# RMSNorm with relu on one core: hardware loops with own semaphores, 32-row chunks in three slots

## The chip, the cores and the metric

One core of one Trainium2 chip. The metric is the device time of one execution in microseconds (us), median of several runs. "Span" is the time from the first to the last instruction in the profile of one execution; it is about 2 us shorter than the device time.

## The reference

```python
def setup_inputs():
    batch, seq, dim = 16, 1024, 512        # x: 16384 rows of 512 float32
    ...
def reference(x, gamma, eps):
    rms = np.sqrt(np.mean(x ** 2, axis=-1, keepdims=True) + eps)
    x_norm = x / rms * gamma
    return np.maximum(x_norm, 0).astype(np.float32)
```

33.55 MB are read and 33.55 MB are written, and little is computed on them.

## The kernel before

128 rows per partition are cut into 8 chunks of 16 rows (one contiguous 32 KB piece per partition), which pass through six slots. A chunk is two groups of 8 rows. SyncE issues all loads and stores of x; ScalarE makes the sums of squares and the square root; VectorE does the rest.

```python
    K = 16; G = 8
    nchunks = rows // K          # 8
    nslots = 6
    junk = psum.tile([P, d], F32, name="junk")       # ONE scratch tile for all squares
    ...
    def compute(i):
        xt = slot[i % nslots]
        for g in range(ngroups):
            a, b = g * G, (g + 1) * G
            for j in range(a, b):
                nc.scalar.activation(out=junk, in_=xt[:, j, :], func=ACTF.Square,
                                     accum_out=ss[i][:, j:j + 1])
            nc.scalar.activation(out=rms[i][:, a:b], in_=ss[i][:, a:b],
                                 func=ACTF.Sqrt, bias=eps_sb, scale=inv_d)
            nc.vector.tensor_mul(out=xt[:, a:b, :], in0=xt[:, a:b, :], in1=gammaG())
            nc.vector.reciprocal(out=rstd[i][:, a:b], in_=rms[i][:, a:b])
            for j in range(a, b):
                nc.vector.tensor_scalar(out=xt[:, j, :], in0=xt[:, j, :],
                    scalar1=rstd[i][:, j:j + 1], scalar2=0.0, op0=ALU.mult, op1=ALU.max)
    # ... gamma: four DMA issues of one row each, then loads and computation of chunks 0 to 5, nxt = 6, then:
    for i in range(nchunks):
        store(i)
        if i >= 1 and nxt < nchunks:
            load(nxt); compute(nxt); nxt += 1
```

Semaphores are placed by the framework, and all of it is straight code.

Of the kernel before, what the change touches and what calls it, by code (L numbers as in the profile page):

```python
# [1 line left out]

# [4 lines left out]

F32 = mybir.dt.float32
ALU = mybir.AluOpType
ACTF = mybir.ActivationFunctionType  # L10


@with_exitstack
def kernel(
    ctx: ExitStack,
    tc: tile.TileContext,
    x: bass.AP,
    gamma: bass.AP,
    eps: bass.AP,
    out: bass.AP,  # L20
):


    nc = tc.nc
    P = nc.NUM_PARTITIONS

    x2 = x.flatten_outer_dims()
    out2 = out.flatten_outer_dims()
    n, d = x2.shape
    rows = n // P  # L30
    inv_d = 1.0 / d
    xv = x2.rearrange("(c p k) d -> c p k d", p=P, k=16)
    ov = out2.rearrange("(c p k) d -> c p k d", p=P, k=16)

    K = 16
    G = 8
    nchunks = rows // K
    nslots = 6
    ngroups = K // G

    singles = ctx.enter_context(tc.tile_pool(name="singles", bufs=1))
    slots = ctx.enter_context(tc.tile_pool(name="slots", bufs=1))
    small = ctx.enter_context(tc.tile_pool(name="small", bufs=1))
    psum = ctx.enter_context(
        tc.tile_pool(name="psum", bufs=1, space=bass.MemoryType.PSUM))

    ctx.enter_context(tc.manual_schedule())

    gseed = singles.tile([P, d], F32, name="gseed")
    gamma_sb = singles.tile([P, d], F32, name="gamma_sb")  # L50
    eps_sb = singles.tile([P, 1], F32, name="eps_sb")
    junk = psum.tile([P, d], F32, name="junk")
    slot = [slots.tile([P, K, d], F32, name=f"slot{s}") for s in range(nslots)]
    ss = [small.tile([P, K], F32, name=f"ss{i}") for i in range(nchunks)]
    rms = [small.tile([P, K], F32, name=f"rms{i}") for i in range(nchunks)]
    rstd = [small.tile([P, K], F32, name=f"rstd{i}") for i in range(nchunks)]

    def load(i):
        nc.sync.dma_start(out=slot[i % nslots], in_=xv[i])

    def store(i):
        nc.sync.dma_start(out=ov[i], in_=slot[i % nslots])

    def gammaG():
        g = gamma_sb[:]
        return bass.AP(tensor=g.tensor, offset=g.offset,
                       ap=[g.ap[0], [0, G], g.ap[1]])

    def compute(i):
        xt = slot[i % nslots]  # L70
        for g in range(ngroups):
            a, b = g * G, (g + 1) * G
            for j in range(a, b):
                nc.scalar.activation(out=junk, in_=xt[:, j, :], func=ACTF.Square,  # L74
                                     accum_out=ss[i][:, j:j + 1])
            nc.scalar.activation(out=rms[i][:, a:b], in_=ss[i][:, a:b],  # L76
                                 func=ACTF.Sqrt, bias=eps_sb, scale=inv_d)
            nc.vector.tensor_mul(out=xt[:, a:b, :], in0=xt[:, a:b, :], in1=gammaG())  # L78
            nc.vector.reciprocal(out=rstd[i][:, a:b], in_=rms[i][:, a:b])  # L79
            for j in range(a, b):  # L80
                nc.vector.tensor_scalar(  # L81
                    out=xt[:, j, :], in0=xt[:, j, :],
                    scalar1=rstd[i][:, j:j + 1], scalar2=0.0,
                    op0=ALU.mult, op1=ALU.max)

    nc.vector.memset(gseed, 0.0)  # L86
    nc.vector.memset(eps_sb, eps)  # L87
    for q in range(0, P, 32):
        nc.scalar.dma_start(out=gseed[q:q + 1, :], in_=gamma[None, :])

    for i in range(min(nslots, nchunks)):
        load(i)
    nc.vector.stream_shuffle(gamma_sb, gseed, [0] * 32)  # L93
    for i in range(min(nslots, nchunks)):
        compute(i)
    nxt = nslots
    for i in range(nchunks):
        store(i)
        if i >= 1 and nxt < nchunks:
            load(nxt)  # L100
            compute(nxt)
            nxt += 1


# [1 line left out]
_INS = ['x', 'gamma', 'eps']  # L106
_OUTS = [((16, 1024, 512), 'float32')]

_NUMBERS = {'eps': 9.999999747378752e-06}


# [26 lines left out]
```

## Time and profile before

| | before |
|---|---|
| device time, median of 3 runs | 164.23 us |
| span | 162.0 us |
| VectorE busy | 124.6 us (77%) |
| ScalarE busy | 98.5 us (61%) |
| DMA engines in packets of x | 96.9% of the span |

The busy share of an engine is an average; what bounds the kernel is read from where a gap would be seen first. The prediction shows those lines (columns of windows: window, length, busy time of VectorE, ScalarE and GpSimd with instruction counts, clock, DMA share, GB/s).

### The profile page before, as it was taken

The page shows a single profiled execution, that of the slowest core. Times are in us where ns is not written, and L with a number is a line of the kernel's source. Part 1 is how long each engine was busy: PE and PEld are TensorE (multiplying, and loading weights), DVE is VectorE, ACT ScalarE, POOL GpSimd, SP SyncE. Part 2 cuts the span into 40 slices and gives each one's busy share as a digit, 9 for nine tenths or more (in the row PEclk, how much of TensorE's full clock was granted, in tenths as well). Part 3 has the DMA queues.
Part 4 walks back from the last instruction along what each step waited for, and adds up shares of the span by engine and source line. Part 5 has one row for each costly group of instructions (what it writes and reads, how often), then busy time and mean ns, then how long its engine had stood idle before and what let it go on. Part 6 is the DMA issues. An engine that isn't in the chain of part 4 may idle for free.

```text
span 162.0 us, 554 instructions
## 1 busy us (share of the span) xinstructions
DVE 124.6 (77%) x164; ACT 98.5 (61%) x274; POOL 0.2 (0%) x4
## 2 busy tenths in 40 slices
DVE  1001299999999999999999999999999999920000
ACT  2107999999999999999999199901998000000000
POOL 0000000000000000000000000000000000000000
DMA  6999899999999999998999999999999999999990
GB/s 227 421 405 502 388 413 493 390 421 477 396 421 471 396 388 388 461 445 388 463 437 404 453 445 404 453 437 396 461 429 445 429 421 445 429 421 445 437 413 16
DMA packets 2315, 67.14 MB, mean 414 GB/s; under 512 B 260, under 2 KB 260, under 8 KB 264
## 3 DMA queue, kind: packets, MB, share of 16 engines
q1 hardware_dynamic: 2304, 67.11, 96.9%
q14 instruction: 3, 0.02, 0.0%
q10 hardware_dynamic: 8, 0.01, 0.0%
HBM read 33.56 MB, written 33.55 MB: 414 GB/s over the span
## 4 chain that ended last, share of the span: by engine, by line
DVE 74%; DMA 8%; ACT 3%; issue 2%; DVEq 0%
DVE slot L78 43%; DVE slot L81 30%; DMA slot<-in_x_dram 8%; ACT junk L74 3%; DVE rstd L79 1%; DVEq L133 0%
## 5 line engine op out<-in xcount | busy, mean ns | idle before, releaser
L74 ACT ACTIVATE junk<-slot 128x512 f32<-128x512 f32 x128 | 76.8, 600 | 23.0 <-DMA slot<-in_x_dram 19.5
L78 DVE TENSOR_TENSOR slot<-slot,gamma_sb 128x4096 f32<-128x4096 f32 x16 | 70.7, 4418 | 4.2 <-ACT junk L74 4.2
L81 DVE TENSOR_SCALAR slot<-slot,rstd 128x512 f32<-128x512 f32 x128 | 52.1, 481 | 0.6
L74 ACT ACTIVATION_READ_ACCUMULATOR junk<-slot 128x1 f32 x128 | 23.8, 186 | 0.0
L93 DVE LOAD_MASK_SELECT gamma_sb<-gseed x1 | 0.0, 14 | 12.8 <-DMA gseed<-in_gamma_dram 12.8
L76 ACT ACTIVATE rms<-ss,eps_sb 128x8 f32<-128x8 f32 x16 | 4.8, 301 | 0.5
L74 ACT ACT_TABLE_LOAD x1 | 1.3, 1283 | 3.2 <-issue 3.2
L79 DVE RECIPROCAL rstd<-rms 128x8 f32<-128x8 f32 x16 | 3.1, 194 | 0.0
L76 ACT ACT_TABLE_LOAD x1 | 1.3, 1283 | 0.0
L86 DVE MEMSET gseed<- 128x512 f32 x1 | 0.5, 485 | 0.9 <-PEq L119 0.9
L93 DVE STREAM_SHUFFLE gamma_sb<-gseed 128x512 f32<-128x512 f32 x1 | 0.7, 721 | 0.0
L119 POOL MEMSET const-bfloat16-1.0<- 128x1 bf16 x1 | 0.1, 101 | 0.0
L119 POOL MEMSET const-uint8-127<- 128x1 uint8 x1 | 0.1, 101 | 0.0
L119 POOL MEMSET const-float32-0.0<- 128x1 f32 x1 | 0.1, 99 | 0.2 <-issue 0.2
L119 POOL MEMSET const-float32-1.0<- 128x1 f32 x1 | 0.1, 98 | 0.0
L87 DVE MEMSET eps_sb<- 128x1 f32 x1 | 0.1, 59 | 0.0
## 6 DMA issues: line engine op xcount, KB each, us to landing
slot<-in_x_dram SPq DMA_DIRECT2D x8, 4096.0 KB, 30.6
out_dram<-slot SPq DMA_DIRECT2D x8, 4096.0 KB, 35.4
gseed<-in_gamma_dram ACTq DMA_DIRECT2D x4, 2.0 KB
```

Of the source, the lines that this page charges most:

```text
L74: nc.scalar.activation(out=junk, in_=xt[:, j, :], func=ACTF.Square, accum_out=ss[i][:, j:j + 1])
L76: nc.scalar.activation(out=rms[i][:, a:b], in_=ss[i][:, a:b], func=ACTF.Sqrt, bias=eps_sb, scale=inv_d)
L78: nc.vector.tensor_mul(out=xt[:, a:b, :], in0=xt[:, a:b, :], in1=gammaG())
L79: nc.vector.reciprocal(out=rstd[i][:, a:b], in_=rms[i][:, a:b])
L81: nc.vector.tensor_scalar(out=xt[:, j, :], in0=xt[:, j, :], scalar1=rstd[i][:, j:j + 1], scalar2=0.0, op0=ALU.mult, op1=ALU.max)
L86: nc.vector.memset(gseed, 0.0)
L87: nc.vector.memset(eps_sb, eps)
L93: nc.vector.stream_shuffle(gamma_sb, gseed, [0] * 32)
L119: nc = _bacc.Bacc("TRN2", target_bir_lowering=False, num_devices=1)
```

## The change

The intent: replace straight code by hardware loops with a few hand-made semaphores, move 64 KB per descriptor instead of 32 KB, fuse the two multiplications, and cut the first and the last chunk so that work starts and ends early. The core of the diff:

```diff
-    K = 16
+    K = 32
-    nslots = 6
+    nslots = 3
-    junk = psum.tile([P, d], F32, name="junk")
+    junk = psum.tile([P, G, d], F32, name="junk")
+    loads = ([(0, 0, G), (0, G, G), (0, 2 * G, K - 2 * G)]
+             + [(i, 0, K) for i in range(1, nchunks - 1)]
+             + [(nchunks - 1, 0, K // 2), (nchunks - 1, K // 2, K // 2)])
+    stores = ([(i, 0, K) for i in range(nchunks - 1)]
+              + [(nchunks - 1, 0, K // 2), (nchunks - 1, K // 2, K // 2)])
 ...
+        for m, (i, a, r) in enumerate(stores):
+            nc.sync.wait_ge(done, i * per + (a + r) // G)
+            store(m)
+            if i == 1:
+                nc.sync.wait_ge(sem_st[0], 16)
+                ... load both halves of chunk 3
+        for m, (i, a, r) in enumerate(loads):          # relay: a landing becomes "ready" counts
+            nc.gpsimd.wait_ge(sem_ld[m], 16)
+            nc.gpsimd.sem_inc(ready, r // G)
 ...
+        with nc.scalar.Fori(0, ngroups) as gi:
+            nc.scalar.wait_ge(ready, 1); nc.scalar.sem_inc(ready, -1)
+            for j in range(G):
+                a = nc.scalar.activation(out=junk[:, j, :], in_=..., func=ACTF.Square, accum_out=...)
+            ... wait sa, Sqrt.then_inc(sq, 1)
+        with nc.vector.Fori(0, ngroups) as gi:
+            nc.vector.wait_ge(sq, 1); nc.vector.sem_inc(sq, -1)
+            nc.vector.reciprocal(...).then_inc(sv, 1)
+            ... wait sv
+            for j in range(G):
+                r = nc.vector.scalar_tensor_tensor(out=row, in0=row, scalar=rstd[...], in1=gamma_sb,
+                                                   op0=ALU.mult, op1=ALU.mult)
+            ... wait sv
+            nc.vector.tensor_scalar_max(out=blk, in0=blk, scalar1=0.0).then_inc(done, 1)
```

Not shown: gamma in one DMA issue with four rows, and the table of the square root loaded ahead.

More of the change, by code (lines that the diff above doesn't have):

```diff
@@ L31 @@
     inv_d = 1.0 / d
-    xv = x2.rearrange("(c p k) d -> c p k d", p=P, k=16)
-    ov = out2.rearrange("(c p k) d -> c p k d", p=P, k=16)
-    K = 16
+    K = 32
     G = 8
     nchunks = rows // K
-    nslots = 6
-    ngroups = K // G
+    nslots = 3
+    ngroups = rows // G
+    per = K // G
+    xv = x2.rearrange("(c p k) d -> c p k d", p=P, k=K)
+    ov = out2.rearrange("(c p k) d -> c p k d", p=P, k=K)
     singles = ctx.enter_context(tc.tile_pool(name="singles", bufs=1))
-    slots = ctx.enter_context(tc.tile_pool(name="slots", bufs=1))
-    small = ctx.enter_context(tc.tile_pool(name="small", bufs=1))
     psum = ctx.enter_context(
         tc.tile_pool(name="psum", bufs=1, space=bass.MemoryType.PSUM))
-    ctx.enter_context(tc.manual_schedule())
     gseed = singles.tile([P, d], F32, name="gseed")
@@ L51 @@
     eps_sb = singles.tile([P, 1], F32, name="eps_sb")
-    junk = psum.tile([P, d], F32, name="junk")
-    slot = [slots.tile([P, K, d], F32, name=f"slot{s}") for s in range(nslots)]
-    ss = [small.tile([P, K], F32, name=f"ss{i}") for i in range(nchunks)]
-    rms = [small.tile([P, K], F32, name=f"rms{i}") for i in range(nchunks)]
-    rstd = [small.tile([P, K], F32, name=f"rstd{i}") for i in range(nchunks)]
-    def load(i):
-        nc.sync.dma_start(out=slot[i % nslots], in_=xv[i])
-    def store(i):
-        nc.sync.dma_start(out=ov[i], in_=slot[i % nslots])
@@ L64, in gammaG @@
-    def gammaG():
-        g = gamma_sb[:]
-        return bass.AP(tensor=g.tensor, offset=g.offset,
-                       ap=[g.ap[0], [0, G], g.ap[1]])
-    def compute(i):
-        xt = slot[i % nslots]
-        for g in range(ngroups):
-            a, b = g * G, (g + 1) * G
-            for j in range(a, b):
-                nc.scalar.activation(out=junk, in_=xt[:, j, :], func=ACTF.Square,
-                                     accum_out=ss[i][:, j:j + 1])
-            nc.scalar.activation(out=rms[i][:, a:b], in_=ss[i][:, a:b],
-                                 func=ACTF.Sqrt, bias=eps_sb, scale=inv_d)
-            nc.vector.tensor_mul(out=xt[:, a:b, :], in0=xt[:, a:b, :], in1=gammaG())
-            nc.vector.reciprocal(out=rstd[i][:, a:b], in_=rms[i][:, a:b])
-            for j in range(a, b):
-                nc.vector.tensor_scalar(
-                    out=xt[:, j, :], in0=xt[:, j, :],
-                    scalar1=rstd[i][:, j:j + 1], scalar2=0.0,
-                    op0=ALU.mult, op1=ALU.max)
@@ L86 @@
-    nc.vector.memset(gseed, 0.0)
-    nc.vector.memset(eps_sb, eps)
-    for q in range(0, P, 32):
-        nc.scalar.dma_start(out=gseed[q:q + 1, :], in_=gamma[None, :])
-    for i in range(min(nslots, nchunks)):
-        load(i)
-    nc.vector.stream_shuffle(gamma_sb, gseed, [0] * 32)
-    for i in range(min(nslots, nchunks)):
-        compute(i)
-    nxt = nslots
-    for i in range(nchunks):
-        store(i)
-        if i >= 1 and nxt < nchunks:
-            load(nxt)
-            compute(nxt)
-            nxt += 1
+    ss = singles.tile([P, rows], F32, name="ss")
@@ new lines @@
+    rms = singles.tile([P, rows], F32, name="rms")
+    rstd = singles.tile([P, rows], F32, name="rstd")
+    slots = singles.tile([P, nslots * K * d], F32, name="slots")
+    junk = psum.tile([P, G, d], F32, name="junk")
[4 more added lines that the diff above has]
+              + [(nchunks - 1, 0, K // 2), (nchunks - 1, K // 2, K // 2)])
@@ new lines, with slot_ap @@
+    sem_ld = [tc.alloc_semaphore(f"ld{i}") for i in range(len(loads))]
+    sem_st = [tc.alloc_semaphore(f"st{i}") for i in range(len(stores))]
+    sem_g = tc.alloc_semaphore("gam")
+    sem_e = tc.alloc_semaphore("epsr")
+    sem_z = tc.alloc_semaphore("zero")
+    ready = tc.alloc_semaphore("ready")
+    sq = tc.alloc_semaphore("sq")
+    done = tc.alloc_semaphore("done")
+    sa = tc.alloc_semaphore("sa")
+    sv = tc.alloc_semaphore("sv")
+    def slot_ap(i):
+        s = (i % nslots) * K * d
+        return slots[:, s:s + K * d].rearrange("p (k d) -> p k d", d=d)
@@ new lines, in load, with store @@
+    def load(m):
+        i, a, r = loads[m]
+        nc.sync.dma_start(out=slot_ap(i)[:, a:a + r, :],
+                          in_=xv[i][:, a:a + r, :]).then_inc(sem_ld[m], 16)
+    def store(m):
+        i, a, r = stores[m]
+        nc.sync.dma_start(out=ov[i][:, a:a + r, :],
+                          in_=slot_ap(i)[:, a:a + r, :]).then_inc(sem_st[m], 16)
+    ctx.enter_context(tc.manual_schedule(engines={mybir.EngineType.SP}))
+    with tc.tile_critical():
+        for m, (i, a, r) in enumerate(loads):
+            if i < nslots:
+                load(m)
+        for m, (i, a, r) in enumerate(stores):
[3 more added lines that the diff above has]
+                nc.sync.wait_ge(sem_st[0], 16)
+                for m2, (c, a2, r2) in enumerate(loads):
+                    if c == nslots:
+                        load(m2)
+        for m, (i, a, r) in enumerate(loads):
+            nc.gpsimd.wait_ge(sem_ld[m], 16)
+            nc.gpsimd.sem_inc(ready, r // G)
+        nc.vector.memset(gseed, 0.0).then_inc(sem_z, 1)
+        nc.vector.memset(eps_sb, eps).then_inc(sem_e, 1)
+        nc.scalar.wait_ge(sem_z, 1)
+        nc.scalar.dma_start(out=gseed[0:P:32, :],
+                            in_=gamma[None, :].to_broadcast([P // 32, d])
+                            ).then_inc(sem_g, 16)
+        nc.scalar.preload_act_table(ACTF.Sqrt)
+        nc.scalar.wait_ge(sem_e, 1)
+        with nc.scalar.Fori(0, ngroups) as gi:
+            nc.scalar.wait_ge(ready, 1)
+            nc.scalar.sem_inc(ready, -1)
+            base = nc.scalar.snap((gi % (nslots * per)) * (G * d))
+            col = nc.scalar.snap(gi * G)
+            for j in range(G):
+                a = nc.scalar.activation(
+                    out=junk[:, j, :], in_=slots[:, bass.ds(base + j * d, d)],
+                    func=ACTF.Square, accum_out=ss[:, bass.ds(col + j, 1)])
+                if j == G - 1:
+                    a.then_inc(sa, 1)
+            nc.scalar.wait_ge(sa, 1)
+            nc.scalar.sem_inc(sa, -1)
+            nc.scalar.activation(out=rms[:, bass.ds(col, G)], in_=ss[:, bass.ds(col, G)],
+                                 func=ACTF.Sqrt, bias=eps_sb, scale=inv_d).then_inc(sq, 1)
+        nc.vector.wait_ge(sem_g, 16)
+        nc.vector.stream_shuffle(gamma_sb, gseed, [0] * 32)
+        with nc.vector.Fori(0, ngroups) as gi:
+            nc.vector.wait_ge(sq, 1)
+            nc.vector.sem_inc(sq, -1)
+            base = nc.vector.snap((gi % (nslots * per)) * (G * d))
+            col = nc.vector.snap(gi * G)
+            blk = slots[:, bass.ds(base, G * d)]
+            nc.vector.reciprocal(out=rstd[:, bass.ds(col, G)],
+                                 in_=rms[:, bass.ds(col, G)]).then_inc(sv, 1)
+            nc.vector.wait_ge(sv, 1)
+            nc.vector.sem_inc(sv, -1)
+            for j in range(G):
+                row = slots[:, bass.ds(base + j * d, d)]
+                r = nc.vector.scalar_tensor_tensor(
+                    out=row, in0=row, scalar=rstd[:, bass.ds(col + j, 1)], in1=gamma_sb,
+                    op0=ALU.mult, op1=ALU.mult)
+                if j == G - 1:
+                    r.then_inc(sv, 1)
+            nc.vector.wait_ge(sv, 1)
+            nc.vector.sem_inc(sv, -1)
+            nc.vector.tensor_scalar_max(out=blk, in0=blk, scalar1=0.0).then_inc(done, 1)
@@ L106 @@
+    with nc.sync.register("landed") as landed:
+        nc.sync.reg_mov(landed, 16)
+        for m in range(len(stores)):
+            nc.sync.wait_ge(sem_st[m], landed)
 _INS = ['x', 'gamma', 'eps']
```

## The prediction

> **What bounds the kernel now.** I read the page first (queues, busy shares), then windows of 18 to 40 us, then the DMA queue's own waits and the timeline, because the busy shares alone point at the wrong engine.
>
> ```profile
> span 162.0 us, 554 instructions
> DVE 124.6 (77%) x164; ACT 98.5 (61%) x274; POOL 0.2 (0%) x4
> ...
> q1 hardware_dynamic: 2304, 67.11, 96.9%
> ...
> DVE 74%; DMA 8%; ACT 3%; issue 2%; DVEq 0%
> ```
>
> The chain that ended last names VectorE for 74%, yet the 16 DMA engines are busy 96.9% of the span with the 67.11 MB that must be moved (33.55 MB in, 33.55 MB out). The windows say which is right:
>
> ```profile
> 2.00:20.00 18.00, 1.65 (x3) 7.99 (x18) 0.00 (x0) 1.00 0.99 421
> ...
> 100.00:140.00 40.00, 39.79 (x53) 17.15 (x49) 0.00 (x0) 1.00 1.00 433
> ...
> 140.00:158.00 18.00, 2.98 (x8) 0.00 (x0) 0.00 (x0) 1.00 1.00 433
> ```
>
> The last two columns are DMA share and GB/s. From 2 to 158 us the DMA has no gap. VectorE ends at 143.0 us, and 15 us of data are still to go: a 4.19 MB store takes 9.8 us at 428 GB/s (67.11 MB in the 157 us from 1.1 to 158), so the DMA queue holds 5 us of backlog when VectorE delivers its last chunk. The bound is the DMA; VectorE is about 5 us from being one.
>
> ```profile
> 0.73 13.13 SPq L59 DMA_DIRECT2D slot<-in_x_dram  x6
> 34.68 15.82 SPq L62 DMA_DIRECT2D out_dram<-slot  x2
> 72.70 0.34 SPq L59 DMA_DIRECT2D slot<-in_x_dram  x1
> ```
>
> These are the queue's issues (start, length). Six loads keep the engines fed until 1.1 + 6 x 9.8 = 60 us. The first store, issued at 34.68, is waited for until 72.70: 60 + 9.8 of its own = 69.8, then some 2 to 3 us to land. So the queue is first in, first out.
>
> ```profile
> L74 ACT ACTIVATE junk<-slot 128x512 f32<-128x512 f32 x128 | 76.8, 600 | 23.0 <-DMA slot<-in_x_dram 19.5
> L78 DVE TENSOR_TENSOR slot<-slot,gamma_sb 128x4096 f32<-128x4096 f32 x16 | 70.7, 4418 | 4.2 <-ACT junk L74 4.2
> L81 DVE TENSOR_SCALAR slot<-slot,rstd 128x512 f32<-128x512 f32 x128 | 52.1, 481 | 0.6
> L76 ACT ACTIVATE rms<-ss,eps_sb 128x8 f32<-128x8 f32 x16 | 4.8, 301 | 0.5
> L79 DVE RECIPROCAL rstd<-rms 128x8 f32<-128x8 f32 x16 | 3.1, 194 | 0.0
> ```
>
> From these rows and the merged chain a group of 8 rows costs VectorE 4.33 (multiply) + 0.12 + 0.02 (reciprocal) + 3.26 (eight scalings) = 7.74 us; 16 groups are 124 us. On ScalarE the squares start every 0.753 us in the timeline, 6.2 us a group.
>
> [...]4418 ns for 4096 elements is 1.08 ns each, and the scalings step by 3.26/8 = 0.407 us for 512.[...]
>
> **The change, part by part.**
>
> *Descriptors.* 1024 of 64 KB take the place of 2048 of 32 KB. A 32 KB one takes 157 x 16 / 2048 = 1.23 us[...].[...]
>
> *VectorE work.* [...] The reciprocal now stands first, 0.19, with a wait, register arithmetic and dispatch behind it: I estimate 0.3 (before, an attached wait cost 0.02). The second wait, before the relu: 0.12. Sum g = 0.19 + 0.3 + 5.46 + 0.12 + 2.21 = 8.3 us a group, against 7.74. I assume that the register arithmetic between the fused operations runs ahead on the sequencer. 16 x 8.3 = 133 us.
>
> *ScalarE.* One table load fewer at the first square root (1.28 us), but the loop waits for its sums: 6.0 + about 0.2 + 0.3 + 0.3 for loop and registers, h = 6.8. It stays below g.
>
> *Start.* The first piece is 2.1 MB: 1.1 + 4.9 + 2.1 (in the kernel before 13.0 - 1.1 - 9.8) = 8.1, with the relay through GpSimd 8.3; plus 6.6 for the first group, VectorE starts at 14.9 instead of 19.1. Gamma should arrive before that: one issue with four rows instead of four issues.
>
> *Order of transfers.* This is what decides. Chunks are 8.39 MB, 19.6 us each, and only three slots exist. Loads 0 to 2 run 1.1 to 60. Store 0 needs 4 groups (48.1), is queued, runs 60 to 79.6. Chunk 1 lands at 42.4 and ScalarE needs 6.8 more, so VectorE begins it at 49.2 and ends it at 49.2 + 4 x 8.3 = 82.4. The queue issuer stands before store 1 and issues the loads of chunk 3 only behind it, so from 79.6 to about 83.2 (0.8 us from issue to data) the DMA is idle: +3.6. Store 1: 83.2 to 102.8. Chunk 3's halves: to 112.6 and 122.4. Its first half is usable at 114.9, squared at 121.5; VectorE, done with chunk 2 at 115.6, idles 6 us. Meanwhile store 2 runs 122.4 to 142.0, store 3a (ready at 138.1) to 151.8. VectorE ends at 121.5 + 4 x 8.3 = 154.7, so the DMA idles another 3.7 us; the last store moves from 155.5 to 165.3.
>
> *End.* From the last data to the end of the span there were 162.0 - 158.0 = 4.0 us: 169.3. Adding 0.3 for the extra blocks at the start[...] gives 168.8, and 164.2 - 162.0 = 2.2 between span and time: **171.0 us**, 4% slower.
>
> So nothing is taken off the bound; the finer first piece gives VectorE 4 us earlier, and this and more is lost because three coarse slots make the last quarter wait load, square, scale and store in turn with little queued behind it.
>
> **Rivals.** (A) *DMA stays full.* If g is 7.0 to 7.4, store 1 is issued before store 0 ends and the last half is ready when store 3a ends; the time is that of before, 164, or 162 to 163 with gains from descriptors. For: the issue order keeps up to 60 us of loads queued; the loop costs are my estimate. Against: [...]at g = 7.7 the same working gives 166.6. (B) *VectorE is the bound outright.* [...] Against: TENSOR_TENSOR at 1.08 ns an element. One in twenty. (C) *The sequencer is the bound.* If register arithmetic and dispatch between two operations take longer than 0.67 us, say 0.8, g is 9.3; time rises by 8 us for each us of g (4 groups of chunk 1 and 4 of chunk 3), so about 179. Nothing in the profile speaks to it, as no register operations stand between the instructions now. One in ten. (D) *Larger descriptors are really faster*, by 2%: -3 us[...].
>
> **Range and chances.** g from 7.8 to 8.8 gives 167 to 175; start and landing times add 1 us either way. Range 166 to 176.5. Faster by over 2% (below 161)[...]: 0.02. Within 2% (to 167.5) needs g below about 7.85 or help from the descriptors: 0.15. Slower: 0.83.
>
> **What would show it.** Right: VectorE's first reciprocal near 15 us; fused operations near 750 ns; relu near 2.3 us; DMA share dropping near 80 to 83 and again near 152 to 155 us; VectorE idle some 6 us before the first group of chunk 3, put down to the square root or the load; last VectorE instruction near 155. Wrong: a DMA share of 1.0 to the end (A)[...], fused operations stepping well above their duration (C), or GB/s above 440 in the store stages (D).

The sum came to 171.0 us. 169.3 + 0.3 made 168.8 with -0.8 for the larger descriptors, an estimate that no run bears out. 5.46 (eight fused operations, each 0.747 us long, 0.673 from one start to the next) and 2.21 (the relu) stand as estimates; the changed kernel's VectorE timeline has 5.39, 0.747, 0.66 and 2.20. That register arithmetic runs ahead of the fused operations was an assumption; there they start every 0.66 us, each before the one ahead of it has ended, with a register operation of 93 to 115 ns for each. ScalarE's 0.2, 0.3 and 0.3 around the root were estimates too; its timeline has 0.19, 0.30 and 0.29. The 0.3 for extra blocks was an estimate that no run tests by itself; the first packet came 0.20 us later than before. The 0.8 us from issue to data were measured as 0.84 (store 1: issued at 81.39, first packet at 82.23).

## More of the kernel before

From windows of one microsecond at the end of the kernel before (columns: window, length, busy time of VectorE, ScalarE and GpSimd with instruction counts, clock, DMA share, GB/s):

```profile
157.00:158.00 1.00, 0.00 (x0) 0.00 (x0) 0.00 (x0) 1.00 0.91 393
158.00:159.00 1.00, 0.00 (x0) 0.00 (x0) 0.00 (x0) 1.00 0.08 33
159.00:160.00 1.00, 0.00 (x0) 0.00 (x0) 0.00 (x0) 1.00 0.08 33
```

33 GB/s in a microsecond is one packet of 32 KB, and a window counts a packet where it starts. From 158 us on a single DMA engine out of 16 still starts packets; the others only finish theirs. The page's list of DMA queues has a line for what is not data:

```profile
q14 instruction: 3, 0.02, 0.0%
```

Three instruction fetches of 8 KB each.

## The result

The changed kernel takes 166.03 us (166.00 to 166.20, 4 runs) against 164.38 us of the kernel before in the same rounds; ratio 1.0106, interval 1.0085 to 1.0128. That is slower by 1%, within the 2% that count as the same. The prediction had 171.0 and 83% for slower by over 2%. 166.03 lies just inside the range of 166 to 176.5, but the loss is a quarter of the one forecast.

From the page of the changed kernel:

```profile
span 164.2 us, 997 instructions
DVE 126.2 (77%) x164; ACT 86.3 (53%) x273; POOL 0.2 (0%) x4
...
q1 hardware_dynamic: 1728, 67.11, 96.7%
...
DVE 1%; issue 0%
```

The DMA has 1728 packets instead of 2304, is busy about as much, and the instruction queue's line is gone. The chain of waits (last line) is of no use here: it stops after the last relu, since the loops' semaphores are counted down by standalone instructions through which it does not follow. So the timeline has to serve. The groups of instructions, which answer to those shown of before (busy time, mean ns of one, idle time before):

```profile
L119 ACT ACTIVATE junk<-slots 128x512 f32 x128 | 74.5, 582 | 44.1 <-ACTq L115 44.1
L143 DVE SCALAR_TENSOR_TENSOR slots<-slots,rstd,gamma_sb 128x512 f32 x128 | 86.2, 747 | 4.8 <-DVEq L140 4.8
L150 DVE TENSOR_SCALAR slots<-slots x16 | 36.7, 2294 | 2.4 <-DVEq L149 0.2
L137 DVE RECIPROCAL rstd<-rms x16 | 3.2, 198 | 11.7 <-DVEq L133 11.7
L126 ACT ACTIVATE rms<-ss,eps_sb x16 | 4.8, 300 | 3.0 <-ACTq L125 3.0
```

The fused operation is 747 ns long and the relu 2294, as predicted. The queue's issues in the timeline (start, length):

```profile
0.94 2.54 SPq L78 DMA_DIRECT2D slots<-in_x_dram  x5
47.46 34.27 SPq L83 DMA_DIRECT2D out_dram<-slots  x2
81.80 1.37 SPq L78 DMA_DIRECT2D slots<-in_x_dram  x2
114.35 38.05 SPq L83 DMA_DIRECT2D out_dram<-slots  x3
```

The second issue of the group that starts at 47.46 is store 1, at 81.39 (so the group ends at 81.73); the last group ends with the last store, issued at 152.06. And VectorE's timeline, at the three moments that count:

```profile
48.30 0.20 DVE L137 RECIPROCAL rstd<-rms  x1 [0.86 <-DVEq L133]
81.27 0.20 DVE L137 RECIPROCAL rstd<-rms  x1
...
118.99 0.20 DVE L137 RECIPROCAL rstd<-rms  x1 [4.66 <-DVEq L133]
...
149.75 2.29 DVE L150 TENSOR_SCALAR slots<-slots  x1
```

Chunk 1 starts at 48.30, chunk 2 at 81.27 and chunk 3 at 118.99; the square brackets show that VectorE waited 0.86 and 4.66 us for ScalarE. From 48.30 to 81.27 are four groups, 8.24 us each.

**Where the 2.2 us of span went.** Windows do not show it: the 16 engines move in step here, a window counts a packet where it starts, and a 64 KB packet lasts 2.4 us, so windows of 1 us give DMA shares of 0.00 and 2.42 in turn. The trace also records each packet by itself. From these records (us from the start of the span; packets of 16 KB and more; "in packets" is the sum of all packet lengths over 16; which packet belongs to which engine is inferred from each starting where another ends):

```
kernel    first packet  all 16 idle                    in packets  last end of 15 engines  of the 16th
before    1.75          never                          156.87      158.05 to 158.95        160.64
changed   1.95          81.43-82.23, 152.37-152.90     158.66      162.65 to 162.79        162.80
```

The last data end 2.16 us later, and the rest after it is 1.4 us in both. The 15 engines end on average at 158.5 and at 162.7, 4.2 us later: the first packet comes 0.20 later; all engines stand idle for 0.80 + 0.53 = 1.33 us; an engine spends 1.79 us more in packets for the same bytes; the remaining 0.9, by difference, is put down to single engines that stop before the others at the gaps. In exchange no engine is left behind: before, the last one ends 2.1 us after that average, now 0.1. The extra packet time is not spread evenly. Where the queue turns from loads to stores or back, packets are longer than their median. In the changed kernel that adds, averaged over the engines, 1.0 us near 58, 0.9 near 99 and 1.0 near 119 to 121 us; in the kernel before 0.7 us near 58 to 61 and next to nothing at later turns.

That gives a theory and its rivals for the experiments. *Theory:* the coarse slots cost the time. Store 1 and the last store come later than the queue lasts, the DMA runs dry twice, and what follows a gap is slow too. *Rivals:* the 64 KB descriptors themselves; VectorE's slower group; the loops. And for the prediction's size: which of its terms were wrong.

### The profile page after: what moved, and what is told of

The parts are those of the page before. It is cut to its first block, busy times and chain, and to the rows that moved or that the text cites. A ratio compares the mean times of both kernels' runs of the same rounds, so it can differ in the third digit from the quotient of the medians.

```text
span 164.2 us, 997 instructions
## 1 busy us (share of the span) xinstructions
DVE 126.2 (77%) x164; ACT 86.3 (53%) x273; POOL 0.2 (0%) x4
## 3 DMA queue, kind: packets, MB, share of 16 engines
q1 hardware_dynamic: 1728, 67.11, 96.7%
## 5 line engine op out<-in xcount | busy, mean ns | idle before, releaser
L119 ACT ACTIVATE junk<-slots 128x512 f32 x128 | 74.5, 582 | 44.1 <-ACTq L115 44.1
L143 DVE SCALAR_TENSOR_TENSOR slots<-slots,rstd,gamma_sb 128x512 f32 x128 | 86.2, 747 | 4.8 <-DVEq L140 4.8
L150 DVE TENSOR_SCALAR slots<-slots x16 | 36.7, 2294 | 2.4 <-DVEq L149 0.2
L119 ACT ACTIVATION_READ_ACCUMULATOR junk<-slots x128 | 23.9, 187 | 0.0
L137 DVE RECIPROCAL rstd<-rms x16 | 3.2, 198 | 11.7 <-DVEq L133 11.7
L126 ACT ACTIVATE rms<-ss,eps_sb x16 | 4.8, 300 | 3.0 <-ACTq L125 3.0
```

The source lines that it names most:

```text
L119: a = nc.scalar.activation(out=junk[:, j, :], in_=slots[:, bass.ds(base + j * d, d)], func=ACTF.Square, accum_out=ss[:, bass.ds(col + j, 1)])
L126: nc.scalar.activation(out=rms[:, bass.ds(col, G)], in_=ss[:, bass.ds(col, G)], func=ACTF.Sqrt, bias=eps_sb, scale=inv_d).then_inc(sq, 1)
L137: nc.vector.reciprocal(out=rstd[:, bass.ds(col, G)], in_=rms[:, bass.ds(col, G)]).then_inc(sv, 1)
L143: r = nc.vector.scalar_tensor_tensor(out=row, in0=row, scalar=rstd[:, bass.ds(col + j, 1)], in1=gamma_sb, op0=ALU.mult, op1=ALU.mult)
L150: nc.vector.tensor_scalar_max(out=blk, in0=blk, scalar1=0.0).then_inc(done, 1)
```

## Experiments

Ten kernels were run, each set beside the kernel before on one chip. All gave the right result but one.

### Smaller descriptors, same order: desc32

```diff
-        nc.sync.dma_start(out=slot_ap(i)[:, a:a + r, :], in_=xv[i][:, a:a + r, :]).then_inc(sem_ld[m], 16)
+        for b in range(a, a + r, min(r, K // 2)):
+            e = b + min(r, K // 2)
+            nc.sync.dma_start(out=slot_ap(i)[:, b:e, :], in_=xv[i][:, b:e, :]).then_inc(sem_ld[m], 16)
```

Stores likewise; waits for a cut transfer count to 32.

> The changed kernel with every 64 KB descriptor cut in two of 32 KB (two issues back to back, the same order, the same waits for both halves). In the trace of the changed kernel packets of 64 KB are slow where the queue turns from loads to stores or back (near 58, 99 and 119 to 121 us), by some 1.0 us on each of the 16 engines at the first two; 32 KB packets at such a turn in the kernel before lost some 0.5 us. Theory T (what is lost at a turn grows with the descriptor): about 1.0 to 1.3 us less than the changed kernel, 164.8 to 165.2 us. Rival D (larger descriptors are a gain of their own, 2418 against 2 x 1213 ns at the median): 0.3 us or more above the changed kernel, 166.3. Rival N (size does not matter, both effects cancel): 166.0.

Measured: 166.15 us, ratio to before 1.0119 (1.0101 to 1.0138), against 1.0106 for the changed kernel. The two idle gaps are there (0.68 and 0.55 us), and the turns lose the same 0.9, 0.8 and 1.0 us. Theory T fell: the loss at a turn does not go with the descriptor. The size of the descriptor, alone, is worth nothing here that these runs can tell from noise: the median packet is 2418 ns for 64 KB and 1213 for 32 KB, 0.3% apart.

### VectorE faster by one microsecond a group: relu_half

```diff
-            blk = slots[:, bass.ds(base, G * d)]
+            half = slots[:, bass.ds(base, G * d // 2)]
-            nc.vector.tensor_scalar_max(out=blk, in0=blk, scalar1=0.0).then_inc(done, 1)
+            nc.vector.tensor_scalar_max(out=half, in0=half, scalar1=0.0).then_inc(done, 1)
```

Wrong result (half of the negative values stay).

> The changed kernel with the relu over only half of each block, so the result is wrong on purpose; VectorE's group shrinks by 1.07 us, from 8.24 to 7.17, nothing else changes. Theory G (the two moments in which all DMA engines are idle, 0.80 us near 81.4 and 0.53 us near 152.4, come from VectorE delivering chunk 1 and the last half too late): both gaps close, 1.0 to 1.6 us less, 164.4 to 165.0 us. Rival V (VectorE's pace sets the time as in the prediction, 8 us for each us of the group): 8.5 us less, 157.5 us. Rival N (gaps do not matter): 166.0.

Measured: 163.11 us, ratio 0.9938 (0.9922 to 0.9954), so 2.9 us less than the changed kernel, about twice what theory G gave, and nowhere near rival V. The relu takes 1227 ns instead of 2294, and a group 7.18 us instead of 8.24. The queue's issues:

```profile
43.30 34.03 SPq L83 DMA_DIRECT2D out_dram<-slots  x2
82.14 0.84 SPq L78 DMA_DIRECT2D slots<-in_x_dram  x2
```

Store 1 is now issued near 77 us, while the queue still has work. In the packet records both gaps are closed (-1.33), and the packet time falls from 158.66 to 157.06 (-1.60): the turns near 99 and 120 us, still in the same order, no longer cost anything to speak of (0.1 in all). So closing the gaps gained more than their own length. That was not in the theory; the last experiment tests it by itself.

### Loops and fused work, but 16-row chunks in six slots: loops16

```diff
-    K = 32
+    K = 16
-    nslots = 3
+    nslots = 6
-    loads = ([(0, 0, G), (0, G, G), (0, 2 * G, K - 2 * G)] ... )
+    loads = ([(0, 0, G), (0, G, G)] + [(i, 0, K) for i in range(1, nchunks)])
 ...
-            if i == 1:
-                nc.sync.wait_ge(sem_st[0], 16)
+            nxt = nslots + i - 1
+            if i >= 1 and nxt < nchunks:
+                nc.sync.wait_ge(sem_st[nxt - nslots], 16)
```

> The hardware loops, own semaphores and fused VectorE work of the changed kernel, but chunks of 16 rows with 32 KB descriptors in six slots, as before; first chunk in two pieces, the last chunk's store in two. VectorE keeps its 8.24 us a group. Theory S (slots and chunk size cost the time, not the loops): no idle gap of the DMA, VectorE ends near 147 us with the queue still full, and since no instruction fetch runs on one DMA engine the last engine ends with the others: 162.5 to 163.5 us, a little under the kernel before. Without that last effect: 164.4. Rival L (the loops and the slower VectorE group cost it): 166.0 as the changed kernel.

Measured: 163.05 us, ratio 0.9936 (0.9919 to 0.9953). Theory S holds, with the last effect as well: this beats the kernel before by 1.1 us, and the changed kernel by 3.0. VectorE's group is the same 8.24 us, so rival L is out. From its page and its timeline:

```profile
span 161.1 us, 1007 instructions
DVE 126.0 (78%) x164; ACT 86.3 (54%) x273; POOL 0.2 (0%) x4
...
q1 hardware_dynamic: 2592, 67.11, 97.6%
...
143.97 2.29 DVE L150 TENSOR_SCALAR slots<-slots  x1
```

VectorE is done at 146.3 us, with 13 us of data still to move. The DMA never stands idle, and the 16 engines end between 158.31 and 159.46 us.

### ScalarE without the shared scratch tile, in the kernel before: before_junk8

```diff
-    junk = psum.tile([P, d], F32, name="junk")
+    junk = [psum.tile([P, d], F32, name=f"junk{j}") for j in range(G)]
-                nc.scalar.activation(out=junk, in_=xt[:, j, :], ...
+                nc.scalar.activation(out=junk[j - a], in_=xt[:, j, :], ...
```

> The kernel before with eight scratch tiles for the squares in place of one, so that no square waits for the one before it. Theory J (the wait for the shared scratch tile set ScalarE's pace of 0.753 us; the prediction carried that pace over to a kernel that has no such wait): squares step by 0.61 us as in the changed kernel, ScalarE's group goes from 6.2 to about 5.3 us, and the time stays at 164.4 within 0.3 us because the DMA is the bound. Rival P (the pace is the operation's own): 0.753 stays.

Measured: 163.82 us, ratio 0.9985 (0.9962 to 1.0007): the same. ScalarE's timeline, two squares that follow each other:

```profile
21.41 0.57 ACT L74 ACTIVATE junk<-slot 128x512 f32<-128x512 f32 x1
21.93 0.18 ACT L74 ACTIVATION_READ_ACCUMULATOR junk<-slot 128x1 f32 x1
22.03 0.57 ACT L74 ACTIVATE junk<-slot 128x512 f32<-128x512 f32 x1
```

They start 0.61 us apart. In the kernel before it was 0.753:

```profile
21.31 0.60 ACT L74 ACTIVATE junk<-slot 128x512 f32<-128x512 f32 x1
21.85 0.19 ACT L74 ACTIVATION_READ_ACCUMULATOR junk<-slot 128x1 f32 x1
22.07 0.60 ACT L74 ACTIVATE junk<-slot 128x512 f32<-128x512 f32 x1
```

In the instruction records of the kernel before, the squares inside a group carry a wait on a semaphore that ScalarE itself counts up after each square; with eight scratch tiles they carry none. So the extra 0.14 us of that pace belonged to the wait, not to the square. Removing it was worth nothing there because the DMA is the bound, but carried over to the changed kernel it misled the prediction.

### ScalarE slowed to the predicted pace: sq10

```diff
+            for j in range(2):
+                nc.scalar.activation(out=junk2[:, j, :], in_=slots[:, bass.ds(base + j * d, d)],
+                                     func=ACTF.Square, accum_out=ss2[:, j:j + 1])
             for j in range(G):
                 a = nc.scalar.activation(
```

> The changed kernel with two more squares per group, to a scratch tile (result unchanged), so ScalarE's group goes from 5.8 to about 7.0 to 7.2 us, near the 6.8 that the prediction carried. VectorE's own work is the same. Theory H (ScalarE's group lies on the path twice, before chunk 1's first group and before chunk 3's, so each us of it costs 2 us): first gap 0.8 grows by 1.3, second likewise, 2.4 to 2.9 us more: 168.5 to 169.0 us. Rival O (ScalarE is off the path, as its 53% share suggests): 166.0.

Measured: 168.41 us, ratio 1.0251 (1.0222 to 1.028), 2.4 us above the changed kernel. VectorE's timeline at the first group of chunks 0, 1 and 3:

```profile
15.49 0.20 DVE L143 RECIPROCAL rstd<-rms  x1 [7.57 <-DVEq L139]
...
49.44 0.20 DVE L143 RECIPROCAL rstd<-rms  x1 [0.88 <-DVEq L139]
...
121.30 0.20 DVE L143 RECIPROCAL rstd<-rms  x1 [5.83 <-DVEq L139]
```

Against 14.37, 48.30 and 118.99 of the changed kernel these are 1.12, 1.14 and 2.31 us later. A group of ScalarE, now some 5.8 + 1.1 = 6.9 us, lies on the path once before chunk 1 and once more before chunk 3. The gaps grow from 0.80 and 0.53 to 1.85 and 1.62 us. Theory H holds, at the lower end of its range, and an engine that was busy for 53% of the changed kernel's span is shown to be on the path.

### VectorE slowed: relu_twice

```diff
-            nc.vector.tensor_scalar_max(out=blk, in0=blk, scalar1=0.0).then_inc(done, 1)
+            nc.vector.tensor_scalar_max(out=blk, in0=blk, scalar1=0.0).then_inc(sv, 1)
+            nc.vector.wait_ge(sv, 1)
+            nc.vector.sem_inc(sv, -1)
+            nc.vector.tensor_scalar_max(out=blk, in0=blk, scalar1=0.0).then_inc(done, 1)
```

> The changed kernel with the relu done twice (result unchanged): VectorE's group goes from 8.24 to about 10.6 us (2.2 and a wait). Theory C (the prediction's order of transfers: in the regime with gaps the time rises 8 us for each us of the group, 4 groups of chunk 1 and 4 of chunk 3): 18 to 19.5 us more, 184 to 185.5 us. Rival V (VectorE's 16 groups in a row set the time, 16 us for each us): 38 us more, 204. Rival N (the DMA bounds): 166 to 170.

Measured: 199.52 us, ratio 1.2143: 33.5 us more. That is a miss for all three, and closest to rival V. The group takes 10.70 us. VectorE's first and last groups:

```profile
14.39 0.20 DVE L137 RECIPROCAL rstd<-rms  x1 [6.23 <-DVEq L133]
...
174.90 0.20 DVE L137 RECIPROCAL rstd<-rms  x1
```

160.5 us between them are 15 groups of 10.70, and VectorE never waits for ScalarE in between. A slope of 8 us for each us of the group could hold only as long as VectorE waits for chunks 1 and 3. Its two waits of the changed kernel, 0.86 + 4.66 = 5.5 us, are used up first, then all 16 groups count: 16 x 2.46 - 5.5 = 33.9, against 33.7 us in the spans (197.9 - 164.2). The prediction's rule of 8 us for each us does not reach this far.

### Three slots with stores in halves: stores16

```diff
-    stores = ([(i, 0, K) for i in range(nchunks - 1)]
-              + [(nchunks - 1, 0, K // 2), (nchunks - 1, K // 2, K // 2)])
+    stores = ([(i, a, K // 2) for i in range(nchunks - 1) for a in (0, K // 2)]
+              + [(nchunks - 1, 0, K // 2)]
+              + [(nchunks - 1, a, G) for a in range(K // 2, K, G)])
-            if i == 1:
+            if i == 1 and a == 0:
                 nc.sync.wait_ge(sem_st[0], 16)
+                nc.sync.wait_ge(sem_st[1], 16)
```

> The changed kernel, three slots and 64 KB loads kept, but each store in halves of 16 rows, the last half in two pieces of 8 rows, and the loads of chunk 3 issued after the first half of store 1. Theory G (the cost is that a store waits for a whole 32-row chunk of VectorE's work, so the DMA runs dry near 81 and 152 us): no idle gap near 81.4, none or under 0.3 us near the end, 163.0 to 163.6 us, as with 16-row chunks. Rival B (three slots are too few whatever the stores): 165 or more.

Measured: 163.17 us, ratio 0.9929 (0.9908 to 0.9951). No idle gap at all, packet time 157.18 us, and the last data at 159.99. So three slots and 64 KB loads are not at fault by themselves. At fault is that a store, and with store 1 the loads of chunk 3 behind it, waits for 32 rows of VectorE's work. (The edit also changes the order: those loads now go ahead of store 1's second half. What each of the two is worth was not tested.) This mends the changed kernel by 2.9 us with a change of one list and one wait, and is as good as loops16 within the spread of the runs.

### The loops written out, 16-row chunks: unrolled16

```diff
-        with nc.scalar.Fori(0, ngroups) as gi:
+        for gi in range(ngroups):
-            base = nc.scalar.snap((gi % (nslots * per)) * (G * d))
+            base = (gi % (nslots * per)) * (G * d)
```

VectorE's loop likewise; all else as loops16.

> The kernel with 16-row chunks in six slots (163.05 us, span 161.1), its two hardware loops written out as straight code; semaphores, order, data and gamma's single issue stay. Theory F (the kernel before ends with one DMA engine 1.2 us behind the next because instruction fetches run on it; the loops take the fetches away): the page shows a queue of kind instruction again, the last engine ends 1 us or more after the others, 164.0 to 164.4 us. Rival M (gamma's four issues on one engine made the straggler): no straggler, 163.0. VectorE's group shrinks by some 0.3 us for want of register work; that lies beside the DMA and is worth nothing.

Measured: 165.15 us, ratio 1.0047 (1.0022 to 1.0073), 2.1 us above loops16; 0.75 us more than the top of theory F's range. (The 1.2 us in the expectation was read from the last two packets, which are of one engine; from engine to engine it is 1.7.) The page again has the instruction queue:

```profile
q14 instruction: 4, 0.03, 0.0%
```

14 of the 16 engines end at 158.50 to 159.41 us, one at 161.06 and one at 162.03. The last one's packets tell how so little traffic costs that much. A fetch at 51.4 us holds the engine for 0.32 us, and its next packet takes 0.65 longer. From then on it is out of step, and at the turns near 60, 91 and 110 us it loses another 1.3, 0.6 and 0.6 us. A second fetch at 129.9 takes 0.30 + 0.35. The kernel before shows the same beginning, a fetch at 50.9 with 0.65 us more on the packet after it, but there the packets can't be followed to its slowest engine without doubt; in before_junk8 the slowest engine's lead back to such a fetch, at 49.9. A fetch alone is not enough: those at 31.9 and 64.9 in unrolled16 cost their engine some 0.3 us and a slower packet, and it is not among the last. The fetches that go with a late engine came 7 to 9 us before the first turn, near 59 us. Why the engine that ends at 161.06 is late stays open; as far as its packets can be followed, no fetch lies on it. Gamma's four issues are not in this kernel, so rival M is out. VectorE's group fell to 8.09 us, for nothing.

### The loops written out, 32-row chunks: unrolled32

The same edit on the changed kernel.

> The changed kernel (three slots of 32 rows) with its two loops written out. With 16-row chunks this took VectorE's group from 8.24 to 8.09 us and brought the instruction fetches back onto the DMA engines (2.1 us slower). Here both count. Theory G+F: store 1 and the last store come 4 x 0.15 = 0.6 us earlier each, so both idle gaps (0.80, 0.53 us) shrink to under 0.3 or close; with a gap closed, the slow packets after it go too; but the engine with the fetches ends late. Between 164.0 and 165.8 us, below the changed kernel's 166.0 in spite of the fetches. Rival L (the loops are a gain in every form, as with 16-row chunks): 167.5 to 168.

Measured: 165.57 us, ratio 1.0077 (1.0059 to 1.0094), within the range of theory G+F, though the slow packets that were to go with the gaps did not go. Against the changed kernel (1.0085 to 1.0128) the intervals overlap, so a gain is not shown. The profiled run was the highest of the seven (167.53; the others 165.42 to 165.96), so only its pattern is used: no moment at which all engines are idle, 15 engines ending together at 162.37 to 162.53, and one at 164.18, whose packets include a fetch at 53.6. The turns near 99 and 120 us stay slow (0.8 and 1.1 us): store 1 still comes just as the queue empties, and the engines still set out together. So the 32-row kernel does not lose by being written out (0.5 us less by the medians), where the 16-row kernel loses 2.1. That the loops' register work (0.15 us a group), which with 32-row chunks delays store 1, eats up what the missing fetches give would explain it; it is argued, not tested by itself.

### One gap made on purpose: gap16

```diff
             if i >= 1 and nxt < nchunks:
+                nc.sync.wait_ge(done, 9)
                 nc.sync.wait_ge(sem_st[nxt - nslots], 16)
```

on loops16.

> The kernel with 16-row chunks in loops (163.05 us, no idle gap), in which the queue issuer now waits for the ninth group before it issues the load of chunk 6: one idle gap of some 8 us near 81 to 89 us, made on purpose, nothing else changed. Theory K (an idle gap lets all 16 engines restart together, and the next turns between loads and stores then hit all of them at once, as near 99 and 120 us of the changed kernel): the time grows by the idle time and 0.8 to 1.6 us more, with slow packets at the turns that follow. Rival I (a gap costs its own length): by the idle time alone, within 0.4 us.

Measured: 173.28 us, ratio 1.0535 (1.0513 to 1.0557). The queue's issues:

```profile
31.17 16.83 SPq L82 DMA_DIRECT2D out_dram<-slots  x2
88.87 0.34 SPq L77 DMA_DIRECT2D slots<-in_x_dram  x1
```

All engines are idle from 81.43 to 89.84, 8.41 us, and the time grows by 10.2 us. The rest is in the packets: 158.84 us instead of 156.99, with 0.7 us lost at the restart near 89 and 1.1 near 98, where loops16 loses none. So this gap costs its length and nearly 2 us more, somewhat above theory K's figure. Rival I is out. Right after the gap all 16 engines set out within some tenths of a microsecond, which fits the picture that a turn costs only where all engines make it at once. Why a turn then takes longer in a packet is not shown by any run.

## Why the prediction was wrong

The order of transfers and its two gaps were foreseen rightly; two terms of the sum, ScalarE's group and the end, were mis-sized. That the time still lies just inside the stated range is owed to the width of the range. Point by point:

- *What bounds the kernel*: right. The DMA; loops16 and relu_half end at the same limit (163.05 and 163.11 us) with VectorE groups of 8.24 and 7.18 us.
- *VectorE's group*, 8.3 us: right, 8.24. The fused operation was put at 0.747 us and measured 0.747; the wait behind the reciprocal at 0.3 and measured 0.30 (0.16 with the loop written out, in unrolled32); the relu at 2.21 and measured 2.2 from its start to the next reciprocal. The relu takes 2294 ns for 4096 elements and 1227 in relu_half for 2048, so 0.521 ns an element by difference. Rivals B and C are out (747 ns, started every 0.66 us); A did not arise, since g was 8.24, and D fell with desc32. (In the prediction's text on rival A, g = 7.7 would give 166.2 by its own 8 us for each us, not 166.6.)
- *Start*: VectorE at 14.9, measured 14.37; the first piece at 8.3, ScalarE's first square at 8.63. Gamma landed in time, at 7.5.
- *Order of transfers*: right in kind. The DMA ran dry before store 1 and before the last store, and VectorE idled before chunk 3 (6 us predicted, 4.66 measured). Wrong in size: 3.6 + 3.7 us of idle DMA were forecast, 0.80 + 0.53 measured.
- **The step that failed first: "h = 6.8".** The squares' pace of 0.753 us was carried over as the cost of a square. Part of it, 0.14 us, was the wait for the one scratch tile, which the changed kernel does not have; the squares follow each other in 0.61 us there. ScalarE's group took 5.8 us. (The working also isn't quite even: the start uses 6.6 for a group, and so does the 121.5; with 6.8 it would be 121.7.) With ScalarE slowed to 6.9, sq10 gives 168.4 us instead of 166.0, and its last data end at 165.1, where the prediction had 165.3. This term is 2.4 of the 5.0 us by which the forecast was too high.
- **The second: "From the last data to the end of the span there were 162.0 - 158.0 = 4.0 us".** That was no fixed cost of an end. 1.4 us are fixed (162.03 - 160.64 before, 164.24 - 162.80 after); the rest was one engine still moving data, late, as unrolled16 makes likely, because of an instruction fetch and what followed it. The changed kernel has no fetches inside its span, and its last gap lets all engines set out together, so the term is 1.4. That is the other 2.6 us: 171.0 - 2.4 - 2.6 = 166.0. That it comes out so evenly is partly luck: the terms +0.3 and -0.8 and the 2.2 us from span to time, which was 1.8 in the changed kernel's profiled run, are wrong too, and nearly cancel.
- *Two errors that nearly cancel.* The data start at 1.95, not at 1.1 as read from a window that counts a packet where it begins, and turns cost about 1 us each, which was not foreseen. So the queue lasted until 81.4 instead of 79.6, which hid part of the idle time: what would have been gap was slow packets instead.
- *Descriptors*, -0.8 us: wrong, nothing (desc32: +0.1, inside the intervals).
- *"8 us for each us of g"*: seen in no run. relu_half gave 2.9 us for 1.06, where the gaps close and the DMA's limit is met, and relu_twice 33.5 for 2.46, where VectorE alone is the bound.

So why did the change not pay? Its parts work against each other. The loops take the instruction fetches off the DMA engines (none in the changed kernel and in loops16, four in unrolled16): with 16-row chunks loops16 is 2.1 us faster than the same kernel written out and, with all else in it, 1.1 us faster than the kernel before. The 32-row stores cost 2.9 us, in two idle gaps and the slow turns that follow them, so that the change ends 1.7 us behind. The larger descriptors are worth nothing (desc32); the fused VectorE work and the earlier start lie beside the bound in loops16, where the DMA never stands idle, but were not tested by themselves. The version without the loss, loops16 at 163.05 us or stores16 at 163.17, beats the kernel before by 0.6 to 0.7% and the changed one by 1.7%.

Open: why a turn between loads and stores costs about 1 us when all engines make it together, why the packet after an instruction fetch is slow, and why some fetches put an engine out of step and others do not.

## What to carry to other kernels

Before a pace read from a profile is carried over to a changed kernel, look at what the instruction waited for; 0.14 us per square was a semaphore that the change removed. Where the DMA is the bound, choose the size of a store by how much work must be done before it can be issued: descriptors of 32 and 64 KB were equal, but a queue that ran dry twice, for 1.3 us in all, cost 2.9. And look at the last engine, not at the mean: in a kernel of 160 us, straight code with four instruction fetches of 8 KB ended 2 us later than loops with none.
